# Where the weight tiles begin in the SBUF partition: byte 96 instead of 64 past a multiple of 128

## The chip, the cores and the metric

The kernel runs on one core of a Trainium2 chip. The time is that of the device for one execution, in microseconds (us); the median of the runs counts.

## What is computed

Two layers of a transformer block on 256 tokens of width 1024, all in float32. Each layer has a wide input projection, three kinds of attention, a gated merge with an output projection, an MLP and a gated extra input:

```python
for i in range(DEPTH):                      # DEPTH = 2
    h = rmsnorm(x, attn_norm[i])
    proj = h @ w_in[i]                      # 1024 x 8004
    (aq, ak, av, bq, bk, bv, cq, ck, cv, iq, ik, iw, gl) = jnp.split(proj, offsets, axis=-1)
    ...
    y_a = diff_attention(...)               # 4 heads, two softmaxes each
    y_b = stick_breaking_attention(...)     # 8 heads
    y_c = dsa_attention(...)                # 8 heads, the 64 best keys of each query
    gates = jax.nn.sigmoid(gl.reshape(b, s, N_BRANCHES, D_MODEL))
    merged = (gates[:, :, 0] * (y_a @ w_br_a[i]) + gates[:, :, 1] * (y_b @ w_br_b[i])
              + gates[:, :, 2] * (y_c @ w_br_c[i]))
    x = x + merged @ w_out[i]
    hm = rmsnorm(x, mlp_norm[i])
    x = x + jnp.square(jax.nn.relu(hm @ w_up[i])) @ w_down[i]      # 1024 x 4096 and back
    hp = rmsnorm(x, ple_norm[i])
    x = x + jax.nn.sigmoid(hp @ w_ple_gate[i]) * (p[i] @ w_ple_proj[i])
```

## The kernel before

**Precision.** Products with weights are made from float32 numbers that are split in two parts of a shorter format (`FR`): a high part, the number rounded, and a low part, the rest. Each product is three matmuls, high x high, high x low and low x high (`mm3`, lines 412 to 415).

**Weights.** `load_unit` (lines 393 to 406) brings 256 rows by 512 columns of a weight matrix as one DMA of 512 KB into a tile `w` [128, 2, 512], from the SP queue. ScalarE copies it to `wh` (rounded), and VectorE, or GpSimd for a few units, subtracts to get `wl`. `w` has 4 buffers, `wh` and `wl` have 6 each, of 4,096 bytes per partition, all in the pool `wp`, one behind the other. So all 16 begin at the same place modulo 128, and so does every piece of 128 columns that TensorE reads, since 128 columns are 512 bytes.

**Matmuls with weights.** There are two forms. In `chunk_T` (442 to 448) with `T_steps` (432 to 440) a [128, 128] piece of `wh` or `wl` is the stationary operand, and 256 columns of activations (all tokens) stream past it; the result is transposed. That is how gates, the b branch's q and k, the branch and output projections, and the MLP are made. Its results are named `mmp`, or `acc` for the down projection, which keeps its sums in four PSUM tiles over all of the MLP. In `chunk` (417 to 430) the activations are stationary and up to 512 columns of weights stream; its results are `mmp` as well. In the profile `mmp<-xh,wh` names both operands whichever is stationary, the streaming one first.

**Activations.** `xh` and `xl` (a normed input), `yh` and `yl` (an attention's or the MLP's inner result) and all other large tiles lie in the pool `sp`.

**Order.** The kernel records its instructions in a `Program`, and a planner with its own table of costs writes them out, engine by engine. Addresses play no part in it: it knows tiles by name.

**Addresses.** Pools are laid out in the order in which they are opened (305 to 311):

```python
    cp = ctx.enter_context(tc.tile_pool(name="cp", bufs=1))
    gap0 = ctx.enter_context(tc.tile_pool(name="gap0", bufs=1))
    wp = ctx.enter_context(tc.tile_pool(name="wp", bufs=6))
    gap1 = ctx.enter_context(tc.tile_pool(name="gap1", bufs=1))
    sp = ctx.enter_context(tc.tile_pool(name="sp", bufs=2))
```

`cp` ends at byte 18,432 of the partition, a multiple of 128. A buffer of the little tiles takes 32 bytes. `gap0` holds the two buffers of `m8` (the eight largest scores), 64 bytes, so that `wp` begins at 18,496, 64 past a multiple of 128. `gap1` behind it holds the four buffers of `ms` and the two of `iw`, 192 bytes, so that `sp` begins at 84,224, a multiple of 128. Tiles in `sp` have sizes that are multiples of 2,048 bytes, so each of them begins at a multiple of 128. Other little tiles lie at the end, in `lp`.

Of the kernel before, what the change touches and what calls it, by code (L numbers as in the profile page):

```python
# [296 lines left out]
def hybrid_block(ctx: ExitStack, tc: tile.TileContext, I, out):  # L297
# [8 lines left out]
# [3 lines that stand above are left out]
    sp = ctx.enter_context(tc.tile_pool(name="sp", bufs=2))  # L309
    mp = ctx.enter_context(tc.tile_pool(name="mp", bufs=1))  # L310
    lp = ctx.enter_context(tc.tile_pool(name="lp", bufs=1))
    gaps = dict(m8=gap0, ms=gap1, iw=gap1)
    pmm = ctx.enter_context(tc.tile_pool(name="pmm", bufs=2, space=PSUM))
    ptr = ctx.enter_context(tc.tile_pool(name="ptr", bufs=2, space=PSUM))
    psc = ctx.enter_context(tc.tile_pool(name="psc", bufs=2, space=PSUM))
# [823 lines left out]
```

## Time and profile before

| | us |
|---|---|
| median of 3 runs (lowest, highest) | 971.93 (969.72, 973.27) |
| the profiled execution | 972.3 |
| its span, first to last instruction | 970.6 |
| TensorE busy: matmuls, loads of the stationary operand | 955.2, 903.1 |
| VectorE, ScalarE, GpSimd busy | 653.9, 539.2, 158.4 |

The span is a little shorter than the execution's time, since the latter takes in what lies before the first and behind the last instruction. Busy times of engines overlap. A matmul's duration in the profile runs from its start to the modelled end of its results, and matmuls are pipelined, so the time that one costs is read from the distance between two starts, or from how many fill a stretch. Nearly all instructions carry the same line, 293, where the planner writes them out; so groups are told apart by the names of their tiles.

### The profile page before, as it was taken

The page shows a single profiled execution, that of the slowest core. Times are in us where ns is not written, and L with a number is a line of the kernel's source. Part 1 is how long each engine was busy: PE and PEld are TensorE (multiplying, and loading weights), DVE is VectorE, ACT ScalarE, POOL GpSimd, SP SyncE. Part 2 cuts the span into 40 slices and gives each one's busy share as a digit, 9 for nine tenths or more (in the row PEclk, how much of TensorE's full clock was granted, in tenths as well). Part 3 has the DMA queues.
Part 4 walks back from the last instruction along what each step waited for, and adds up shares of the span by engine and source line. Part 5 has one row for each costly group of instructions (what it writes and reads, how often), then busy time and mean ns, then how long its engine had stood idle before and what let it go on. Part 6 is the DMA issues. An engine that isn't in the chain of part 4 may idle for free.

```text
span 970.6 us, 18469 instructions
## 1 busy us (share of the span) xinstructions
PE 955.2 (98%) x7506; PEld 903.1 (93%) x7506; DVE 653.9 (67%) x1009; ACT 539.2 (56%) x770; POOL 158.4 (16%) x137
## 2 busy tenths in 40 slices
PE   8899999999999999999999999999999999999998
PEld 7888889999999999999989788898999999999997
DVE  7749897674766555567686599975557755655573
ACT  6547674475455544556564576645845545554462
POOL 1202122324220000001321102231252100000010
PEclk9999999999999999999999999999999999999999
DMA  8664245636666666566556543556265665666551
GB/s 272 201 215 126 84 154 171 180 124 198 194 173 200 193 195 196 174 190 207 152 161 184 182 136 113 154 173 195 90 212 167 188 214 176 181 202 211 191 173 44
DMA packets 89194, 168.59 MB, mean 174 GB/s; under 512 B 5722, under 2 KB 9236, under 8 KB 89108
## 3 DMA queue, kind: packets, MB, share of 16 engines
q1 hardware_dynamic: 89108, 167.40, 55.4%
q8 instruction: 59, 0.97, 0.4%
q14 instruction: 27, 0.22, 0.1%
HBM read 166.33 MB, written 1.05 MB: 172 GB/s over the span
## 4 chain that ended last, share of the span: by engine, by line
PE 91%; DVE 4%; ACT 2%; issue 1%; DMA 1%; SPq 0%; POOL 0%; DVEq 0%; ACTq 0%
PE mmp L293 66%; PE acc L293 18%; PE z L293 2%; PE sc L293 2%; DVE wl L293 1%; DVE qo L293 1%; DMA w<-in_w_in 1%; PE qps L293 1%; ACT wh L293 1%; PE ob L293 1%; PE oc L293 1%; PE pps L293 1%; DVE io L293 1%; DMA xin<-in_x 0%; PE xps L293 0%
## 5 line engine op out<-in xcount | busy, mean ns | idle before, releaser
L293 ACT ACTIVATE wh<-w 128x1024 fp32r<-128x1024 f32 (+2 forms) x318 | 330.6, 1045 | 201.2 <-PE mmp L293 98.4
L293 DVE TENSOR_TENSOR wl<-w,wh 128x1024 fp32r<-128x1024 f32 (+1 forms) x284 | 342.1, 1213 | 146.9 <-ACT wh L293 141.6
L293 PE MATMUL mmp<-xh,wh 128*128 128x256 f32 x1088 | 304.4, 280 | 2.8 <-DVE rm L293 2.8
L293 PE MATMUL mmp<-xl,wh 128*128 128x256 f32 x1088 | 304.2, 280 | 0.0
L293 PE MATMUL mmp<-xh,wl 128*128 128x256 f32 x1088 | 303.8, 279 | 0.0
L293 PEld LDWEIGHTS mmp<-xh,wh 128*128 128x128 f32 x1088 | 205.2, 189 | 4.2 <-issue 3.1
L293 PEld LDWEIGHTS mmp<-xl,wh 128*128 128x128 f32 x1088 | 204.6, 188 | 1.1 <-issue 0.7
L293 PEld LDWEIGHTS mmp<-xh,wl 128*128 128x128 f32 x1088 | 204.7, 188 | 0.1
L293 PE MATMUL acc<-yh,wh 128*128 128x256 f32 x512 | 141.5, 276 | 0.0
L293 PE MATMUL acc<-yh,wl 128*128 128x256 f32 x512 | 141.4, 276 | 0.0
L293 PE MATMUL acc<-yl,wh 128*128 128x256 f32 x512 | 141.4, 276 | 0.0
L293 POOL TENSOR_TENSOR wl<-w,wh 128x1024 fp32r<-128x1024 f32 x34 | 87.6, 2577 | 201.0 <-ACT wh L293 201.0
L293 PE MATMUL mmp<-wh,xh 128*128 128x512 f32 (+2 forms) x296 | 113.4, 383 | 0.9 <-ACT av L293 0.7
L293 PE MATMUL mmp<-wh,xl 128*128 128x512 f32 (+2 forms) x296 | 112.7, 382 | 0.0
L293 PE MATMUL mmp<-wl,xh 128*128 128x512 f32 (+2 forms) x296 | 112.1, 380 | 0.0
L293 PEld LDWEIGHTS acc<-yh,wh 128*128 128x128 f32 x512 | 96.1, 188 | 0.0
L293 PEld LDWEIGHTS acc<-yl,wh 128*128 128x128 f32 x512 | 96.1, 188 | 0.0
L293 PEld LDWEIGHTS acc<-yh,wl 128*128 128x128 f32 x512 | 96.1, 188 | 0.0
L293 PE MATMUL mmp<-yl,wh 128*128 128x256 f32 x336 | 93.3, 279 | 0.2
L293 PE MATMUL mmp<-yh,wh 128*128 128x256 f32 x336 | 93.3, 278 | 0.2 <-ACT pp L293 0.2
L293 PE MATMUL mmp<-yh,wl 128*128 128x256 f32 x336 | 93.0, 278 | 0.0
L293 POOL TENSOR_TENSOR rsq<-ms,half 128x8 f32<-128x8 f32 (+3 forms) x30 | 47.0, 1572 | 222.4 <-DVE ms L293 222.4
(196 smaller groups left out, 1193.1 us busy)
## 6 DMA issues: line engine op xcount, KB each, us to landing
w<-in_w_in SPq DMA_DIRECT2D x118, 512.0 KB, 4.0
w<-in_w_up SPq DMA_DIRECT2D x64, 512.0 KB, 3.7
w<-in_w_down SPq DMA_DIRECT2D x64, 512.0 KB, 4.5
w<-in_w_out SPq DMA_DIRECT2D x16, 512.0 KB, 4.5
w<-in_w_ple_gate SPq DMA_DIRECT2D x16, 512.0 KB, 3.7
w<-in_w_br_a SPq DMA_DIRECT2D x8, 512.0 KB, 5.1
w<-in_w_br_c SPq DMA_DIRECT2D x8, 512.0 KB, 4.4
w<-in_w_br_b SPq DMA_DIRECT2D x8, 512.0 KB, 4.2
```

The source lines that it names most:

```text
L293: getattr(self.engines[op.eng], op.name)(*op.args, **op.kw)
```

## The change

One line. `gap0` now holds the three buffers of `mx` (the row maxima of a softmax) in place of the two of `m8`, 96 bytes; `gap1` holds the three of `nb` (minus the maxima times the scale) and the two of `iw`, 160 bytes, in place of `ms` and `iw`. `m8` and `ms` go to `lp`.

```diff
-    gaps = dict(m8=gap0, ms=gap1, iw=gap1)
+    gaps = dict(mx=gap0, nb=gap1, iw=gap1)
```

So `wp` begins at 18,528, 96 past a multiple of 128, and every buffer of `w`, `wh` and `wl` is moved by 32 bytes. `sp` begins at 84,224 as before, and no large tile moves. Of the little ones `m8`, `ms`, `mx`, `nb`, `iw`, `rs0` and some of `lp` lie elsewhere. Instructions, their order on each engine and their semaphores are the same.

## Rows read from the trace of the kernel before

**Rows 1.** The page: the span, and each engine's busy time, share and instructions.
```profile
span 970.6 us, 18469 instructions
...
PE 955.2 (98%) x7506; PEld 903.1 (93%) x7506; DVE 653.9 (67%) x1009; ACT 539.2 (56%) x770; POOL 158.4 (16%) x137
```
**Rows 2.** The page's chain that ended last: shares by engine, then by line.
```profile
PE 91%; DVE 4%; ACT 2%; issue 1%; DMA 1%; SPq 0%; POOL 0%; DVEq 0%; ACTq 0%
PE mmp L293 66%; PE acc L293 18%; PE z L293 2%; PE sc L293 2%; DVE wl L293 1%; DVE qo L293 1%; DMA w<-in_w_in 1%; PE qps L293 1%; ACT wh L293 1%; PE ob L293 1%; PE oc L293 1%; PE pps L293 1%; DVE io L293 1%; DMA xin<-in_x 0%; PE xps L293 0%
```
**Rows 3.** Groups by form: shape, count | busy us, mean ns | idle before, releasers.
```profile
L293 PE MATMUL mmp<-xh,wh 128*128 128x256 f32 x1088 | 304.4, 280 | 2.8 <-DVE rm L293 2.8
...
L293 PE MATMUL acc<-yh,wh 128*128 128x256 f32 x512 | 141.5, 276 | 0.0
...
L293 PE MATMUL mmp<-wh,xh 128*128 128x512 f32 x248 | 98.6, 398 | 0.2 <-ACT xh L293 0.2
...
L293 PEld LDWEIGHTS acc<-yh,wh 128*128 128x128 f32 x512 | 96.1, 188 | 0.0
...
L293 PE MATMUL mmp<-yh,wh 128*128 128x256 f32 x336 | 93.3, 278 | 0.2 <-ACT pp L293 0.2
```
**Rows 4.** The chain in order of time: start us, us, what, matmuls in it.
```profile
220.36 34.88 PE mmp L293 x306
...
316.37 10.88 PE mmp L293 x96
...
698.50 34.88 PE mmp L293 x306
```
**Rows 5.** The same from the w_out projection on, first and second layer.
```profile
272.98 15.66 PE mmp L293 x133
...
749.93 16.84 PE mmp L293 x143
```
**Rows 6.** The same for the last projection, weights streaming.
```profile
943.63 11.11 PE mmp L293 x48
```
**Rows 7.** Stretches: us, busy PE, PEld, DVE, ACT, POOL, then PEclk, DMA share, GB/s.
```profile
310.00:457.00 147.00, 147.00 (x1299) 147.00 (x1298) 83.93 (x86) 73.26 (x87) 1.97 (x3) 1.00 0.61 193
790.00:935.00 145.00, 145.00 (x1281) 145.00 (x1281) 82.58 (x85) 71.60 (x85) 1.83 (x3) 1.00 0.61 192
271.00:286.50 15.50, 15.50 (x134) 15.50 (x134) 13.38 (x18) 9.57 (x15) 5.01 (x6) 1.00 0.62 173
```
**Rows 8.** Timeline of TensorE in that last stretch: start us, us, instruction.
```profile
285.18 0.28 PE L293 MATMUL mmp<-xh,wh 128*128 128x256 f32 x1
285.30 0.28 PE L293 MATMUL mmp<-xl,wh 128*128 128x256 f32 x1
```
**Rows 9.** Little tiles: count: duration ns least/median/most, first and last start.
```profile
L293 DVE SCALAR_TENSOR_TENSOR nb<-mx,rsq x12: 150/154/168, 122.3 to 687.2; 128x4 f32<-128x4 f32 x8, 128x8 f32<-128x8 f32 x4
...
L293 DVE TENSOR_SCALAR ms<-hss x20: 139/158/167, 27.7 to 653.2; 128x8 f32<-128x8 f32 x16, 128x1 f32<-128x1 f32 x4
```
**Rows 10.** DMA issues: count, KB each, median us from issue to landing.
```profile
w<-in_w_in SPq DMA_DIRECT2D x118, 512.0 KB, 4.0
w<-in_w_up SPq DMA_DIRECT2D x64, 512.0 KB, 3.7
w<-in_w_down SPq DMA_DIRECT2D x64, 512.0 KB, 4.5
```
**Rows 11.** What ScalarE waits for before it writes wh: us, times, longest.
```profile
ACT wh L293 <- PE mmp L293: 98.4, 117, 6.0
...
ACT wh L293 <- PE acc L293: 64.3, 55, 3.0
...
ACT wh L293 <- DMA w<-in_w_in: 7.3, 8, 2.0
```
**Rows 12.** The split in the first up and down stage, 310 to 457 us.
```profile
L293 ACT ACTIVATE wh<-w x55: 1046/1063/1067, 309.5 to 456.9; 128x1024 fp32r<-128x1024 f32 x55
L293 DVE TENSOR_TENSOR wl<-w,wh x54: 1211/1224/1226, 310.6 to 454.6; 128x1024 fp32r<-128x1024 f32 x54
```

## The prediction, made before the result was known

> **What bounds the kernel now.** I read the page's busy lines first [rows 1]: TensorE is busy 955.2 of 970.6 us, and the loads of its stationary operand 903.1. The chain of waits says the same [rows 2]: 91% of it is TensorE, of which `mmp` 66% and `acc` 18% are the matmuls with weights; VectorE has 4%, ScalarE 2%, DMA 1%. So what matters is how many ns TensorE takes from the start of one weight matmul to the start of the next. I call this the pace.
>
> The groups by form give the counts [rows 3]. In 5,808 matmuls a piece of a weight tile is the stationary operand and 256 columns of activations stream past it: 3 x 1,088 of `mmp<-xh/xl`, 3 x 512 of `acc<-yh/yl` and 3 x 336 of `mmp<-yh/yl`. In 888 the activations are stationary and the weights stream; 744 of these have 512 columns. The 512-column ones have a pace of 11.11 us / 48 = 231.5 ns [rows 6].
>
> The 256-column ones have two paces at one and the same placement. In the up and down projections the chain's pieces are 96 matmuls in 10.88 us, 113.3 ns each [rows 4]. In the w_out projection and the up projection behind it they are 133 in 15.66 us, 117.7 ns, and in the second layer 143 in 16.84 us, 117.8 ns [rows 5]. Both are steady over tens of us, both layers show them at the same place in the program, and the granted clock is 1.00 in both stretches [rows 7], so it is not the clock. Nor is it a wait: in the timeline of the long pace matmul follows matmul with no idle time between [rows 8]. I call them the short and the long pace. The reader should see that something which is not in the instruction stream moves TensorE by 3.9%, and that the address of the weights modulo 128 is not that something by itself, since it is 64 in both.
>
> **The change part by part.** It adds and removes no instruction; order and waits of every engine stay. It moves the 16 weight buffers by 32 bytes (byte 18,496 to 18,528 for the first), and little buffers of 64 to 128 bytes to other places. The large activation tiles stay at multiples of 128. So each term is (count) x (change of one duration).
>
> *Little buffers.* `nb` (12 instructions) lies in three buffers, at 32, 64 and 96 modulo 128, and takes 150 to 168 ns; `ms` (30; the 20 shown) in four, at all four places, and takes 139 to 167 ns [rows 9]. The spread over all places is under 30 ns. With 32 reads and writes of `m8` each and 12 of `mx`, some 120 VectorE instructions could change by that: at most 120 x 0.028 = 3.4 us either way if all lay on the path. VectorE has 4% of the path, so 0.1 us. I take 0: TensorE's own work covers it. Without that cover it would be the 3.4 us.
>
> *Weight loads.* A load lands 4.0 us after its issue, 3.7 to 4.5 by its source [rows 10]; the ring of four buffers is refilled well ahead, and ScalarE waits for weights only 7.3 us in all [rows 11]. Half of that spread between sources is a tenth of 4.0 us; if a changed start in SBUF made loads a tenth longer or shorter, the exposed wait would change by 0.7 us. I take 0 and keep +/- 0.7. If the cover of the ring were gone, each load would show its tenth, 0.4 us, to ScalarE; that is rival 3.
> The Trainium skill has a rule against the change here ("DMA: Bandwidth & Descriptors", "How a descriptor splits into AXI transactions"): a descriptor that doesn't start at a multiple of 256 bytes begins at the boundary below, and the bytes before its start cost beats of 32 bytes. If it holds for the SBUF side, 2 KB rows that start at 96 instead of 64 cost 67 beats instead of 66; as an estimate from that page 1.5% of 4.0 us, and by it the sum would be 0.1 us more. No run here shows it.
>
> *Splitting.* ScalarE rounds w to wh, VectorE (for a few units GpSimd) subtracts to wl. All three tiles move together. In the up and down stage 55 of ScalarE's take 1,046 to 1,067 ns and 54 of VectorE's 1,211 to 1,226, a spread of at most 2% with everything else running [rows 12]; I bound a shift by the same 2%. These lines are about 2% of the chain (DVE wl and ACT wh, 1% each [rows 2]), 19 us, so +/- 0.4 us. I take 0. If they did become late, TensorE's weight load would be what waits.
>
> *TensorE.* The stationary operand's row of 512 bytes moves from 64 to 96 past a multiple of 128 while the moving operand's stays at 0; in the 888 the roles are exchanged. No row shows weights at 96. Bound from both sides by the two paces. How many matmuls run at each: at the short pace at least 1,299 + 1,281 in the two up/down stages (147.0 and 145.0 us, 113 ns each [rows 7]) and most of the two pieces of 306 in 34.88 us (114.0 ns [rows 4]), 3,192 together. At the long pace at least 133 + 143 = 276 [rows 5]. The remaining 2,340 lie between. All to the long pace: between 3,192 x 4.4 ns = +14.0 us and 5,532 x 4.4 = +24.3 us; the middle is +19. All to the short pace: between 276 x 4.4 = -1.2 us and 2,616 x 4.4 = -11.5 us; the middle is -6.4. For the 744 wide ones no second pace is read; with the same 3.9% of 231.5 ns they move by +/- 6.7 us.
> I take 0, since the nearest rows are those of the stages themselves: the same operand addresses gave both paces, both layers fell into the same one at the same place although the weights stood in other slots of the ring, so what selects the pace seems to be how a stretch of matmuls begins, not where the weights lie. 96 is a multiple of 32 as 64 is.
>
> Sum: 972.3 + 0 = **972.3 us**. This is on the profiled execution's own time, which holds 1.7 us around its span of 970.6; the median of the three runs is 971.9, 0.4 lower.
>
> A rule on the same term: the Trainium skill says that TensorE's two reads of SBUF, moving and stationary, have independent ports, and that TensorE and ScalarE never wait on anyone ("SBUF — State Buffer", "Who interferes with whom"). By this the term is exactly 0. The trace does not quite bear it out: a TensorE that never waited would not show two paces with the same operands and no instruction in between.
>
> **The rivals.**
> 1. *The short pace is lost* (slower). The short pace would then be a lucky meeting of the two streams that TensorE reads, at a distance of 64 bytes modulo 128, and 96 would miss it. For: the pace has discrete values, so it depends on some relation in time between streams, and 32 bytes of the moving stream are 8 of its 256 columns, 3.5 ns at the short pace, which is close to the 4.4 ns that separate the paces. Against: the long pace exists at 64 too. It decides as soon as the up and down stage no longer shows 10.88 us per 96. Price +19 us: 991 us; if only half of the stages lose it, 982.
> 2. *The short pace is found everywhere* (faster). The same relation, on the lucky side: the stretches at 117.7 ns fall to 113.3. For: the long pace costs something today, and nothing else keeps TensorE. Against: at most 2,616 matmuls can gain. -6.4 us, and with a quarter of the wide matmuls' 6.7 us, -8: 964 us.
> The Trainium skill gives a further step in that direction ("TensorE: Matmul & The Clock Gate", "Back-to-back issue gap"): 262 cycles for 256 columns, 109.2 ns at 2.4 GHz. By it the sum would be, as an estimate, 972.3 - 3,192 x 4.1 ns - 2,616 x 8.5 ns = 937 us. No weight matmul of the trace runs at that pace, and I give it 2 in 100 of the faster case.
> 3. *Weights come late* (slower). Loads or the split take longer than the bounds above by several times, at the start and where a gate's weights are needed. For: 32 past a multiple of 64 is a start that no large tile has had so far. Against: the slack of ScalarE, which waits 98 and 64 us for TensorE to release wh buffers [rows 11], and not the other way round. If one load in twenty (15 of some 300) showed its 0.4 us in full: +6, 978 us.
> That the change does not do what it says can be left out: the addresses follow from the sizes of the pools.
>
> **How the numbers follow.** 0.5% of this time is 4.9 us, about what a measurement of this kernel can tell from no change. No change in the paces: 0.34, within 4.9 us. Short pace lost, in whole or in part: 0.30. Weights late: 0.05. Short pace everywhere: 0.31. So faster 0.31, same 0.34, slower 0.35. The first is the likeliest by little, and its own range is 968 to 977. The cases of both signs hold most of the chance, so the range has to reach to both: 961 (rival 2 with all of its 11.5 us) to 991 (rival 1 at its middle); what is left out is the fuller loss, the wide matmuls on top, and the step to 109 ns.
>
> **What the profile after would show.** If I am right: pieces of 96 matmuls in 10.88 us in the up and down stage, 117.7 ns in the w_out stretch, and 231.5 ns for the 512-column ones, with LDWEIGHTS at 188 ns [rows 3]. Rival 1: the pieces of 96 at 11.3 us. Rival 2: the w_out stretch at 113.3. Rival 3: TensorE's busy time as before and idle time before its weight loads, released by ScalarE or VectorE. What would make the prediction wrong is above all that the address does select the pace; then the sign is decided by which stretches change.

## The result, and the profile after

The changed kernel takes **994.5 us** (median of 4 runs, 993.3 to 994.6), the kernel before 972.6 in the same comparison: a ratio of 1.022, 95% interval 1.0205 to 1.0238. It is slower by 21.9 us. The forecast of 972.3 was wrong, and the range ended 3.5 us below the result. What came is rival 1, the lost short pace, a little dearer than its price of 19 us.

The page after, its busy lines and the shares of the chain:

```profile
span 992.8 us, 18469 instructions
...
PE 978.7 (99%) x7506; PEld 923.9 (93%) x7506; DVE 653.0 (66%) x1009; ACT 540.3 (54%) x770; POOL 158.3 (16%) x137
...
PE 93%; DVE 3%; DMA 2%; ACT 1%; issue 0%; SPq 0%; POOL 0%; ACTq 0%; DVEq 0%
```

Set beside [rows 1]: the span grew by 22.2 us, TensorE's busy time by 23.5 with the same 7,506 matmuls. VectorE, ScalarE and GpSimd have the busy time that they had, to 1.1 us. So the time is inside TensorE's own work, not in a wait for another engine.

Groups of the trace after, by form (shape, count | busy us, mean ns | idle before), against [rows 3]:

```profile
L293 PE MATMUL mmp<-xh,wh 128*128 128x256 f32 x1088 | 308.5, 284 | 2.6 <-DVE rm L293 2.6
...
L293 PE MATMUL acc<-yh,wh 128*128 128x256 f32 x512 | 143.4, 280 | 0.0
...
L293 PE MATMUL mmp<-wh,xh 128*128 128x512 f32 x248 | 99.6, 401 | 0.0
...
L293 PEld LDWEIGHTS acc<-yh,wh 128*128 128x128 f32 x512 | 96.2, 188 | 0.0
```

Each matmul is 3 to 4 ns longer in these groups, and LDWEIGHTS has its 188 ns still. A matmul's own duration overlaps the next; the pace is read from the chain in order of time (start us, us, what), against [rows 4 to 6]:

```profile
311.23 11.27 PE acc L293 x96
322.50 11.27 PE mmp L293 x96
...
713.28 42.08 PE mmp L293 x357
...
965.49 11.31 PE mmp L293 x48
```

A piece of 96 now takes 11.27 us, 117.4 ns a matmul, where it took 10.88. The pieces of the gates, 42.08 / 357 = 117.9, have left the 114.0. The wide ones went from 231.5 to 235.6 ns. And the pieces show no short pace in any stage. The granted clock is not the cause; the same stretches as in [rows 7] have it at 1.00, the upper of its two levels (2.4 GHz), with fewer matmuls in them (1,255 for 1,299, and 1,238 for 1,281):

```profile
310.00:457.00 147.00, 147.00 (x1255) 147.00 (x1254) 79.72 (x79) 70.55 (x79) 0.00 (x0) 1.00 0.61 192
790.00:935.00 145.00, 145.00 (x1238) 145.00 (x1238) 79.38 (x81) 69.82 (x80) 0.00 (x0) 1.00 0.60 186
```

Nor do weights land later; from issue to landing (against [rows 10]):

```profile
w<-in_w_in SPq DMA_DIRECT2D x118, 512.0 KB, 3.9
w<-in_w_up SPq DMA_DIRECT2D x64, 512.0 KB, 3.7
w<-in_w_down SPq DMA_DIRECT2D x64, 512.0 KB, 4.4
```

And ScalarE's rounding into `wh` takes what it took (1,059 ns before as well):

```profile
L293 ACT ACTIVATE wh<-w 128x1024 fp32r<-128x1024 f32 x306 | 322.4, 1059 | 212.1 <-PE mmp L293 99.6 <-PE acc L293 71.7 <-issue 26.7
```

The loss can be added up. I took the time from one matmul's start to the next wherever two weight matmuls of the same width are neighbours in the trace, up to 125 ns for 256 columns and 250 for 512; longer ones (80 of 5,779 before) are left out. With 256 columns the mean of some 5,700 pairs rose from 114.38 to 117.52 ns: 5,808 x 3.14 = 18.2 us. With 512 columns it rose from 229.82 to 233.38: 744 x 3.56 = 2.6 us. The 96 with 324 columns add 96 x 3.1 = 0.3. The sum is 21.1 of the 21.9 us. What is left fits the granted clock: three of the four runs of the changed kernel had a mean clock of 0.996 (994.5 to 994.6 us), and the runs of the kernel before on record at 0.996 took 973.4 to 974.8, in the mean 974.1. At the same mean clock the change costs some 20.5 us.

### The profile page after: what moved, and what is told of

Its sections match the earlier page's. It is cut to its first block, busy times and chain, and to the rows that moved or that the text cites. A ratio compares the mean times of both kernels' runs of the same rounds, so it can differ in the third digit from the quotient of the medians.

```text
span 992.8 us, 18469 instructions
## 1 busy us (share of the span) xinstructions
PE 978.7 (99%) x7506; PEld 923.9 (93%) x7506; DVE 653.0 (66%) x1009; ACT 540.3 (54%) x770; POOL 158.3 (16%) x137
## 3 DMA queue, kind: packets, MB, share of 16 engines
HBM read 166.33 MB, written 1.05 MB: 169 GB/s over the span
## 4 chain that ended last, share of the span: by engine, by line
PE 93%; DVE 3%; DMA 2%; ACT 1%; issue 0%; SPq 0%; POOL 0%; ACTq 0%; DVEq 0%
PE mmp L293 68%; PE acc L293 18%; PE z L293 2%; PE sc L293 2%; DMA w<-in_w_in 1%; DVE qo L293 1%; PE qps L293 1%; DVE wl L293 1%; PE ob L293 1%; PE oc L293 1%; PE pps L293 1%; ACT wh L293 1%; DVE io L293 1%; DMA xin<-in_x 0%; DVE rm L293 0%
## 5 line engine op out<-in xcount | busy, mean ns | idle before, releaser
L293 PE MATMUL mmp<-xh,wh 128*128 128x256 f32 x1088 | 308.5, 284 | 2.6 <-DVE rm L293 2.6
L293 PE MATMUL mmp<-xl,wh 128*128 128x256 f32 x1088 | 308.2, 283 | 0.0
L293 PE MATMUL mmp<-xh,wl 128*128 128x256 f32 x1088 | 307.9, 283 | 0.0
```

Source lines behind the costliest of these rows:

```text
L293: getattr(self.engines[op.eng], op.name)(*op.args, **op.kw)
```

## The experiments

The theory to test: what sets the pace is the **distance** in the partition between the starts of TensorE's two operands (weight past activation for the narrow matmuls): 64 bytes before, 96 after. Its rivals: the little buffers' places; loads into 96 or the split of tiles there; the weights' own address. Each edit is to the kernel before. All these kernels keep the instructions of each engine.

**e1, little buffers alone.** `m8` and `ms` lie at the end and `mx`, `nb` and `iw` in the gaps, as in the change, but for `mx` and `iw`, which exchange their gaps; the weights stay at 64.
```diff
-    gaps = dict(m8=gap0, ms=gap1, iw=gap1)
+    gaps = dict(iw=gap0, mx=gap1, nb=gap1)
```


> Weights stay at 64; m8 and ms lie at the end, mx and nb in the gaps, as in the changed kernel. Theory A (TensorE's pace depends on where the stationary and the streaming operand begin, and nothing else of the change counts): 972 us as before, pieces of 96 matmuls in 10.88 us. Theory C (the little buffers or what depends on them cost the time): 980 to 994 us, with the pieces at 10.88 us.


Measured: 972.3 us, ratio 1.0001 (0.9987 to 1.0015). The little buffers cost nothing.

**e2 and e5, only `w` at 96.** The loaded tiles get a pool of their own at 96; `wh` and `wl` stay at 64 modulo 128. In e2 they were shifted by 128 bytes on the way; e5 has them at 64 modulo 512 as before.
```diff
+    wp = ctx.enter_context(tc.tile_pool(name="wp", bufs=6))
+    gapw = ctx.enter_context(tc.tile_pool(name="gapw", bufs=1))
+    wld = ctx.enter_context(tc.tile_pool(name="wld", bufs=4))
...
+        w = prog.tile(wld, [P, 2, n], F32, "w", tag="w", bufs=WB, padded_shape=[P, 2, 512])
```


> Only the landing tiles w begin at 96; wh and wl, which TensorE reads, stay at 64. Theory A: 972 us, pieces of 96 in 10.88 us. Theory D (loads into, or ScalarE's and VectorE's reads of, tiles at 32 past a multiple of 64 are slower): over 980 us, with longer wh, wl or landings than 1,059 ns, 1,232 ns and 4.0 us.

> Only the loaded weights w lie at 96 modulo 128 (in a pool of their own); their halves wh and wl lie at 64, at the same place modulo 512 as in the kernel before, and so do the activations. If the distance between the two operands that TensorE reads sets the pace: as the kernel before, 972 us within 3, pieces of 96 matmuls in the up and down stage at 10.9 us. If loads into 96 or the reading of w at 96 by ScalarE, VectorE and GpSimd are the cause: 990 to 995, pieces of 96 at 11.3 us. The first run with w alone gave 993, but there wh and wl had also moved by 128 bytes; if this run is at 972, that step of 128 bytes cost the 20 us, and the distance counts modulo 256 and not modulo 128.


Measured: e2 993.0 us, ratio 1.020 (1.018 to 1.023); e5 972.2 us, ratio 0.9992 (0.9979 to 1.0004). By e2 alone I should have blamed loads and split; the second answer was the other one. Both load and read `w` at 96, and in both ScalarE's wh takes 1,058 ns, as before (1,059). So e5 excludes loads and split, and the two differ by where `wh` and `wl` lie, 128 bytes apart: the distance does not count modulo 128. ScalarE in e5, then the chain of e2, then that of e5:

```profile
L293 ACT ACTIVATE wh<-w 128x1024 fp32r<-128x1024 f32 x306 | 322.0, 1058 | 194.1 <-PE mmp L293 103.9 <-PE acc L293 64.8 <-issue 19.8
```

```profile
322.82 11.31 PE mmp L293 x96
```
```profile
316.75 10.88 PE mmp L293 x96
```

**e3, weights at 96 and activations at 32.** The distance is 64 again.
```diff
+    gaps = dict(mx=gap0, ms=gap1, iw=gap1)
```


> Weights at 96 as in the changed kernel, and all large activation tiles at 32 past a multiple of 128 instead of 0, so the distance is 64 again. Theory A1 (only the distance of the two operands modulo 128 counts): 972 us, pieces of 96 in 10.88 us, wide matmuls 231.5 ns. Theory A2 (the address of the weights itself counts): 994 us, pieces in 11.27 us. If neither distance nor weights alone count, something else, say 976 to 990 us.


Measured: 982.5 us, ratio 1.0105 (1.0076 to 1.0135), half of the loss, and what neither the theory of the distance (972) nor that of the weights' own address (994) gave. The chain says which half:

```profile
219.90 34.87 PE mmp L293 x306
...
304.52 11.31 PE acc L293 x96
315.83 11.31 PE mmp L293 x96
```

The gates are back at 114.0 ns, as in [rows 4]; the up and down stage sits at 117.8, the long pace of [rows 5]. So the distance makes the short pace possible but does not ensure it. e11 takes that up.

**e4 and e7, bare stretches.** TensorE alone, VectorE copying one result out per stretch. The loop as e7 has it; in e4 the two starts are `4 * a` and `4 * b` in place of `sb // 4` and `mb // 4`.
```diff
+        for i in range(count):
+            s0 = sb // 4 + 128 * (i % 4)
+            m0 = mb // 4 + 256 * (i % 2 if n == 256 else 0)
+            nc.tensor.matmul(out=ps[:, 0:n], lhsT=st[:, s0:s0 + P], rhs=mv[:, m0:m0 + n],
+                             start=i == 0, stop=i == count - 1, skip_group_check=True)
```


> Not the reference's computation: stretches of matmuls alone on TensorE, 48 with 256 streaming columns and 24 with 512, for each start of the stationary and the streaming operand from 0 to 112 past a multiple of 128 in steps of 16 bytes; no other engine at work. Theory A1: the pace is the same along a diagonal (equal distance modulo 128), 113.3 or 117.7 ns at distance 64 and 117.3 ns at distance 96, and differs between diagonals. Theory A2: it is the same along a row of equal stationary start. If the paces of the kernel come from other engines' accesses to SBUF: one pace everywhere, near 109 ns.

> Leaves out the whole computation: only stretches of 48 matmuls, 128x128 by 256 columns in fp32r, at 32 distances of the stationary operand's start past the streaming one's (0 to 496 in steps of 16 bytes), six times over in six orders. If the distance counts modulo 256, the 113.3 ns show at 64 and at 320 alike, and not at 192 and 448; if modulo 128, at 64, 192, 320 and 448; if modulo 512 at 64 alone. At 96 the pace should be 116.5 to 119 ns every time. If the pace is by chance, each distance shows both paces over the six.


Measured in e4: 113.33 ns at distance 64 in seven of eight readings, 116.7 to 120.0 at most other pairs. (113.33 came also at distance 144 in both readings and at 192 in two of eight.) In e7 the six readings at 64 and the six at 320 (64 modulo 256) were 113.33; at 192 and 448 one of six, the others 117.8. At 96 they were 117.3 or 118.8, at 0 120.0, at 32 118.33, at 208 116.67, and each place in the upper 256 bytes gave the values of its partner in the lower, mostly reading by reading. So the distance counts **modulo 256**, as far as the stationary start goes, which alone moves in e7. It does not say all: in e4 two operands at distance 0 took 120.0 and 119.8 ns with both starts at 0, 116.7 and 118.3 with both at 16. At 64 the four pairs of starts agreed but for that one reading of eight; the pair 96 and 32, which e3 has, ran at 113.33 in both, so its starts as such did not keep e3's up and down stage at the long pace. Chain of e7: stretches of 48 at 64, 96, 320, 352 (the last two letters name the distance: first 64s, then 16s):

```profile
30.32 5.44 PE d_ba L46 x48
41.46 5.70 PE d_bc L46 x48
...
120.97 5.44 PE d_fa L46 x48
132.11 5.70 PE d_fc L46 x48
```

48 in 5.44 us are 113.3 ns, 48 in 5.70 are 118.8, with no wait in between and no other engine at work but for VectorE's one copy per stretch.

**e6, weights at 96, of the activations only `yh` and `yl` at 32.** Two distances in one run.
```diff
+    yp = ctx.enter_context(tc.tile_pool(name="yp", bufs=3))
...
+        return tuple(prog.tile(yp, [P, 4, SEQ], FR, n, tag=n, bufs=3) for n in ("yh", "yl"))
```


> Weights at 96 as in the change, and of the activations only yh and yl moved to 32 modulo 128, xh and xl stay at 0. If the distance of the operands sets the pace, the matmuls that stream yh and yl (distance 64) can run at 113.3 ns and those that stream xh and xl (distance 96) stay at about 117.3 in the same run: 2,544 matmuls gain up to 4.0 ns each, so 984 to 994 us, the chain's pieces of 96 at 10.9 for acc and 11.3 for mmp in the up and down stage, if the pace can change within a stage. If the weights' own address decides, all stay at 117.3 and 994.5 us.


Measured: 991.3 us, ratio 1.019 (1.017 to 1.021). The chain of the first layer's up and down stage, then the second's:

```profile
309.86 10.90 PE acc L293 x96
320.76 11.26 PE mmp L293 x96
332.03 10.90 PE acc L293 x96
342.93 11.26 PE mmp L293 x96
...
817.04 11.30 PE acc L293 x96
828.35 11.39 PE mmp L293 x96
```

In the first layer the pace changes with every piece: down projections (`acc` streams yh, yl, distance 64) at 113.5 ns, up projections (distance 96) at 117.3, same weights' place, same clock, same engines at work. So the weights' own address does not decide. In the second layer the up projections stand at 118.6, the other pace of distance 96 in the map, and behind them `acc` falls into its long one, 117.7.

**e8 and e9, weights at 0 and at 32.** `gaps = dict()` without gap pools; and `ms` and `nb` in `gap1` with 32 bytes of filler in `gap0`.


> All weights at 0 modulo 128, activations at 0 modulo 512 (distance 0). The map of stretches showed 116.7 to 120 ns at distance 0. If the distance sets the pace: 5,532 matmuls at about 118 ns, 990 to 997 us, near the change, with the wide matmuls of 512 columns between 227 and 236 ns (plus or minus 5 us). If the weights' address alone counts and 96 is what is bad about the change: 972.

> All weights at 32 modulo 128, activations at 0, distance 32. A forecast from the maps of bare stretches alone: at distance 32 they took 118.33 ns in all eight readings, against a mean of 114.4 in the kernel before, 5,808 x 3.95 = 22.9 us; wide matmuls with the stationary start at 0 and the streaming one at 32 took 233.3 against 229.8 in the kernel before, 744 x 3.5 = 2.6 us. Together 972.7 + 25.5 = 998 us within 3. If the maps don't carry over to the kernel: 972 (only 96 is bad) or another place.


Measured: e8 1001.8 us, ratio 1.029 (1.028 to 1.031), above the expected range; e9 995.8, ratio 1.0235 (1.022 to 1.025), against a forecast of 998. The paces came as the maps had them: at 32, means of 118.30 ns and 233.25 for the wide ones (maps 118.33 and 233.3); at 0, 119.92 and 227.84 (maps 116.7 to 120 in e4 and 120.0 in e7, and 226.7). For distance 0 I had put 118, a middle over starts; the pair with both starts at 0, which is the kernel's, had shown 120.0 and 119.8 in e4. Chain at 0, then at 32:

```profile
324.00 11.52 PE mmp L293 x96
...
973.86 11.00 PE mmp L293 x48
```
```profile
321.29 11.36 PE mmp L293 x96
```

**e10, finer steps.**


> Leaves out the whole computation: stretches of 48 matmuls of 256 columns at distances 0 to 252 in steps of 4 bytes, twice, and of 24 matmuls of 512 columns at 0 to 240 in steps of 16. If the short pace is a narrow meeting of two streams, it shows at 64 and few places around it; if finer steps hide a still shorter pace, some distance shows less than 113.3 ns, and a faster kernel could be made of it. At multiples of 16 the values of the map before should come back.


Measured: the short pace sits at few and narrow places. 113.33 ns came at 52 and 76 twice, at 64, 88 and 168 once in two readings; 56, 60, 68 and 72 gave 117.8 to 119.7. The slowest were 133.3, at 28, 32 and 36, three stretches in a row, in the first reading and not in the second. Nothing was under 113.3. Most multiples of 16 repeated e7; 32 and 48 did not in one reading each (133.3 and 123.3), and 64 was at 117.8 in its second.

**e11, the way in.**


> Leaves out the whole computation: 96 stretches of 48 matmuls at distance 64, each behind a stretch of 46 to 51 matmuls at another of 16 distances. If the way in selects between 113.3 and 117.8 ns at distance 64, some of the 96 show 117.8, and which ones depends on the stretch before (its distance, its length). If distance 64 always gives the short pace when nothing else works, all 96 show 113.3, and the long pace in the kernel must come from other work there.


Measured: of the 96 stretches at distance 64, 66 ran at 113.33 ns and 30 at 117.8. Behind distance 0 all six were long; behind 48, 64, 128, 144 and 240 all were short; behind the other ten it changed with the number of matmuls in the stretch before (each pair of distance and number ran once). The stretches at 64 behind 0 (`t_aa`), and behind 64 (`t_ea`), each following its `p`:

```profile
7.80 5.51 PE p_aa L46 x46
13.32 5.65 PE t_aa L46 x48
...
51.83 5.21 PE p_ea L46 x46
57.04 5.44 PE t_ea L46 x48
```

All the timed kernels by mean pace, and the change in us that these means give with the counts of above (5,808 and 744; distances of narrow matmuls modulo 256; run by run, against 972.0 to 973.5 of the kernel before):

| weights past activations | 256 columns, ns | 512 columns, ns | by the paces | measured |
|---|---|---|---|---|
| 64 (before) | 114.38 | 229.82 | 0 | 0 |
| 64 (e1) | 114.25 | 229.88 | -0.7 | +0.3 |
| 64 (e5) | 114.12 | 229.82 | -1.5 | -0.5 |
| 64, both moved (e3) | 116.18 | 229.45 | +10.2 | +10.5 |
| 64 for y, 96 for x (e6) | 117.21 | 233.27 | +19.0 | +18.6 |
| 96 (the change) | 117.52 | 233.38 | +20.9 | +21.9 |
| 192 (e2) | 117.55 | 233.35 | +21.0 | +21.0 |
| 32 (e9) | 118.30 | 233.25 | +25.3 | +22.4 |
| 0 (e8) | 119.92 | 227.84 | +30.7 | +29.1 |

The paces account for each kernel within 3 us. Part of what is left is again the granted clock: three of e9's four runs had 1.000 (995.1 to 996.1 us), at which the kernel before took 969.8 to 972.7, in the mean 971.1, so some 24.5 us for the 25.3. None of these kernels beats the one before: with every narrow matmul at 113.33 it would gain 5,808 x 1.05 = 6 us, but no edit was found that makes every stretch enter the short pace, and e5, the best at distance 64, is level with it.

## Why the prediction was wrong

- **Little buffers, 0: right** (e1, within 0.15%).
- **Weight loads and splitting, 0: right** (e5, and the trace after). Landings are 3.7 to 4.4 us, and ScalarE's wh is at 1,059 ns. The Trainium skill's rule of AXI beats ("DMA: Bandwidth & Descriptors", "How a descriptor splits into AXI transactions") would have made loads into 96 some 1.5% longer, as an estimate; at 3.9, 3.7 and 4.4 us for 4.0, 3.7 and 4.5 the trace does not show it, nor in the packets of 2,048 bytes, the weights' rows, which took 104.1 ns in the mean for 104.4.
- **TensorE, 0: wrong.** The step that failed is "what selects the pace seems to be how a stretch of matmuls begins, not where the weights lie. 96 is a multiple of 32 as 64 is." It took one of two causes for the only one. How a stretch begins does choose between 113.3 and 117.8 ns (e11, e3), but only where the distance offers both; at 96 the maps have 116.7 to 120.0 and no short pace. I had read "the same operand addresses gave both paces" as the address not mattering, though every row had one address and so could not vary it. That the second layer's weights stood in other slots was no evidence either: slots are 4,096 bytes apart, the same place modulo 256.
- **The bounds on TensorE's term held, the range did not.** The term was bounded at +14.0 to +24.3 us for the narrow matmuls and +6.7 for the wide; it measured 18.2 and 2.6. The range left out the wide ones on top of rival 1, and those 2.6 us are most of the 3.5 by which the result lies outside. Of rival 1's reason the distance of 64 is borne out by the maps, though modulo 256 and not 128; that the two streams meet in time is not shown. Nor do the 3.5 ns that 32 bytes of the stream last explain the 4.4 between the paces: in e10 one column, 4 bytes, is enough (at 60 119.5 and 119.7 ns, at 64 113.3 in one reading of two, at 52 and 76 in both). Rival 1's sign, pieces of 96 at 11.3 us, came.
- **Rivals 2 and 3: fell.** No stretch at 96 found the short pace, and loads and split kept their times. The 109.2 ns that the Trainium skill gives for 256 columns ("TensorE: Matmul & The Clock Gate", "Back-to-back issue gap") came nowhere: nothing in e10 is under 113.3. The section gives it for an isolated matmul, so it was no forecast for these stretches, in which every matmul has a weight load.
- The rule of the Trainium skill that TensorE never waits on anyone ("SBUF — State Buffer", "Who interferes with whom") gave a term of 0 too. The bare stretches show that 0 does not follow for the pace: with the same instruction it is 113.3 to 120 ns at most places, by the operands' starts and the way in. Whether one of TensorE's reads then waits for the other is not shown.

Why these distances, and what in TensorE or the SBUF the two reads meet in, no run shows; the entry's rule beyond the table of e11 is open as well. The maps are means over the second half of each stretch.

## What to carry to other kernels

Where TensorE streams back to back, the starts of stationary and moving tile belong to its price: here 32 bytes were worth 2.2% (to 96) and 2.4% (to 32), 64 bytes 2.9% (to 0). Fix their distance modulo 256 and map it with bare stretches of the kernel's own matmul, at two entries at least; for the narrow matmuls at 32 and at 0, where the maps of e7 have one pace only, they carried over to the kernel within 0.1 ns (the wide ones at 0 ran 1.1 ns longer than in the map). And when one address shows two paces, that does not say that the address is free: vary it before leaving it out of the sum.

## What was not expected of the hardware

Some distances have two steady paces or more, and after its first matmuls a stretch keeps the one it has entered: 64 (113.33 and 117.8), 96 (117.3 and 118.8, in e11 behind stretches at 64 also 120.0), 144 (116.67 and 120.0), 192 (113.33 and 117.8). And 512 streaming columns meet other paces than 256: in e10 they ran at 226.67 ns at distance 0, where 256 columns are among the slowest (120.0), and at 233.3 at most others. So the two widths of this kernel want different distances; in the kernel, with the roles of weights and activations exchanged, the wide ones ran at 227.84 ns at 0 (e8) and 229.82 before.
